# Seven inner products for the block product A12·B21 of an up-projection in one-level Strassen form

## The chip, the cores and the metric

The kernel runs on one core of a Trainium2 chip. The metric is the device time of one execution in microseconds: the median of three runs. The core's engines each run their own instruction stream: PE (TensorE, the matrix products), DVE (VectorE), ACT (ScalarE), POOL (GpSimd) and SP (SyncE, here the issuer of most DMAs). [...]

## The reference

One inference step of a hybrid streaming encoder layer, in float32: 1024 new frames of one stream (with 16 meta tokens ahead) and 32 frames of a running stream. What matters here is the feed-forward at the layer's end:

```python
def conv_ffn(x, gate_past, g, w_up, dw_w, dw_b, w_down):
    h = rmsnorm(x, g)
    u = h @ w_up                       # (tokens, 1024) @ (1024, 5632)
    gate, up = u[..., :D_FF], u[..., D_FF:]
    gate_ext = jnp.concatenate([gate_past, gate], axis=1)
    y = jax.nn.silu(depthwise_causal_conv(gate_ext, dw_w, dw_b)) * up
    return x + y @ w_down, gate_ext[:, -(FFN_CONV_WIDTH - 1):]
```

The gate passes a causal convolution of width 3 along the tokens, then silu, and multiplies the other half. D_FF is 2816, that is 22 tiles of 128 channels.

## The kernel before

**Products in float32.** Every factor is kept as two reduced-precision parts, `hi` (a cast) and `lo` (the rest, `raw - hi`), and a product is three matmuls into one PSUM bank: hi·hi, hi·lo, lo·hi. The helper `hilo` does such a split: a cast on ACT (line 1218), then a subtraction on DVE (line 1219). x after the second norm's weights is in `BH`, `BL`.

**Tiles.** The up-projection runs over f = 0 to 21, 128 channels of the gate and 128 of the other half each. Tiles 0 and 1 are plain products. From tile 2 on each tile is a 2 x 2 block product in Strassen's form (Winograd's variant): the weights' rows are the two halves (gate, other), their columns the two halves of the 1024 inputs; x is cut along the inputs and, within each of two parts of the tokens (p = 0, 1), into two blocks of tokens. Seven products instead of eight: product 1 is A11·B11, product 2 is A12·B21, and both add up to the gate of the first block of tokens; the rest use sums of blocks. `THI`, `TLO` hold the sums of x for products 5, 6, 7. Each product is done for both parts, so that a tile has 14 half products (q, p), each of 4 x 3 matmuls into a bank of 264 columns, or 268 for products 1 and 2 at p = 0 (four more tokens ahead of it). `SEQ_` gives the order 1, 5, 6, 2, 7, 3, 4; `BANK` puts products 1, 6, 7 and 4 one after the other into the same bank (they accumulate), 5 and 3 into a second, 2 into a third. After each half product its bank is added to one of the four blocks: the first write of a block is an ACT copy (line 1422), the later ones are DVE additions (line 1424). Tile 21 has the order `SEQL`: 1, 6, 7, 5, 3, 2, 4.

**Weights.** While tile f's products run, the generator `w_forms` prepares the weights of tile f + 1: it loads three pieces `b`, `a`, `g` (line 1244; 256, 256 and 512 KB), builds the sums on DVE (lines 1249, 1250, 1255, 1258) and splits each by `hilo` into buffers from the list `free`.

**The gate chain.** After product 3 of the second part, `gate_done` runs: a multiply on DVE (line 1338), two small POOL copies, a multiply-add (1341), two more (1344), silu on ACT (1347), a multiply (1348). `y_done` then multiplies with the other half (1353, 1354) and, for tiles 2 to 17, stores y and sums of its blocks for the down-projection (`t1` to `t4`, lines 1373 and 1381 to 1383; stores at 1365). Even tiles keep their gate in `X[2]` (in rows of the trace `x`, in rows of the program's order `x_2299`) and y in `rb`; odd tiles keep the gate in `gx` and y in `X[0]` (`x_2297`). `X[1]` (`x_2298`) holds the raw weights. `gate_start` (line 1334) writes two values of the state ahead of each tile on POOL.

**Order.** PE's order is that of the code. DVE, ACT, POOL and SP are ordered by a scheduler when the program is built.

**The step to the down-projection.** During tile 21 the function `first_hook` feeds what the first down-projection products (`d_mm`, lines 255 to 257 and 1625) read: y of tiles 0 and 1 (`arow`, into `th`, `tl`) and two blocks of `wdn`, `wa[1]` first needed and `wa[0]` needed later (both into `bh`, `bl`, 1024 columns). The loads are issued by the class `Feed` (line 1527), and each is split by `hilo`.

Of the kernel before, what the change touches and what calls it, by code (L numbers as in the profile page):

```python
# [169 lines left out]
def body(nc, tc, cp, wp, xp, dp, io):  # L170
# [1032 lines left out]
    with tc.tile_pool(name="psB", bufs=1, space=PSUM, reuse_waits="tile") as pf:  # L1203
# [34 lines left out]

        def w_forms(key, src, raws):
            w = ups[key] = Up()  # L1240
            g, a, b = raws
# [8 lines left out]
            tt_(out=a, in0=g[:, A], in1=a, op=ALU.subtract)  # L1250
# [99 lines left out]
        def y_done(f):  # L1350
# [134 lines left out]
        for i, (u, p, c) in enumerate(((0, 1, 0), (0, 1, 1), (0, 0, 0), (1, 1, 0), (1, 1, 1), (0, 0, 1), (1, 0, 0), (1, 0, 1))):  # L1485
# [3 lines left out]
            if i == 4:  # L1489
# [408 lines left out]
```

## Time and profile before

| | us |
|---|---|
| three timed runs: median (lowest to highest) | 1048.96 (1048.79 to 1049.0) |
| the profiled execution's own time | 1049.94 |
| its span, first to last instruction | 1048.2 |
| PE busy | 1030.8 |
| DVE busy | 864.8 |
| ACT busy | 506.6 |
| POOL busy | 163.0 |

The span is from the first to the last instruction of the profiled execution; its own time is that of the same execution as the timer gives it. The busy time of an engine is the sum of its instructions. The mean granted clock of TensorE was 0.999. Tile 2 begins at 393 us, tile 21 at 782, and the down-projection at 803.

### The profile page before, as it was taken

To read this page: it belongs to the slowest core of one execution; us is meant where nothing else is said; L and a number is where in the kernel's file an instruction comes from. 1 tells how busy PE (TensorE), PEld (TensorE's weight loads), DVE (VectorE), ACT (ScalarE), POOL (GpSimd) and SP (SyncE) were. 2 spreads that over 40 slices of the span, in tenths; PEclk is the share of its full clock that TensorE was granted. 3 is DMA by queue.
4 is the path that set the end of the run, shared out by engine and by line. 5 is a ranking of instruction groups with operands and counts; after the bars stand their busy time and mean duration, and the time that the engine had idled before them with its cause. 6 is when DMAs were issued, how large, how long until landed. Compare 5 with 4: busy or idle time off the path is not lost.

```text
span 1048.2 us, 19994 instructions
## 1 busy us (share of the span) xinstructions
PE 1030.8 (98%) x7747; PEld 1004.9 (96%) x7747; DVE 864.8 (83%) x1649; ACT 506.6 (48%) x1074; POOL 163.0 (16%) x205
## 2 busy tenths in 40 slices
PE   9999999989999999999999999999999999999997
PEld 8999998758999999999999999999999999999997
DVE  7999988899978978888887888888777976986636
ACT  8653336896676744433333443343336722532334
POOL 1133220002325220001000000110010041000043
PEclk9999999999999999999999999999999999999999
DMA  7378673124963123243233233332426795832204
GB/s 268 90 170 163 146 152 81 41 54 70 174 151 108 61 71 102 72 141 96 72 110 125 63 103 109 97 103 76 130 63 207 250 194 132 249 123 69 94 2 166
DMA packets 69047, 124.41 MB, mean 119 GB/s; under 512 B 10448, under 2 KB 42568, under 8 KB 68952
## 3 DMA queue, kind: packets, MB, share of 16 engines
q1 hardware_dynamic: 56392, 97.77, 29.2%
q0 software_dynamic: 12128, 24.95, 14.1%
q8 instruction: 61, 1.00, 0.4%
q10 hardware_dynamic: 432, 0.41, 0.1%
q14 instruction: 34, 0.28, 0.1%
HBM read 79.42 MB, written 27.51 MB: 102 GB/s over the span
## 4 chain that ended last, share of the span: by engine, by line
PE 88%; ACT 6%; DVE 3%; DMA 2%; issue 1%; DVEq 0%; ACTq 0%
PE mm L1282 55%; PE mm L255 10%; PE mm L256 10%; PE mm L257 10%; ACT pb L764 1%; DVE acc L403 1%; ACT glu L828 1%; DMA raw<-woc 1%; PE R L292 1%; ACT hi L341 1%; PE R L271 1%; DMA xs<-xT 0%; ACT glu L764 0%; ACT pb L774 0%; DMA prm<-prm 0%
## 5 line engine op out<-in xcount | busy, mean ns | idle before, releaser
L1282 PE MATMUL mm<-bh,sl 128*128 128x264 f32 (+1 forms) x912 | 214.0, 284 | 0.0
L1282 PEld LDWEIGHTS mm<-bh,sl 128*128 128x128 f32 x912 | 157.2, 188 | 0.0
L403 DVE SCALAR_TENSOR_TENSOR acc<-glu,prm,acc 128x324 f32<-128x324 f32 (+4 forms) x190 | 155.0, 844 | 1.1
L1282 PE MATMUL mm<-bl,sl 128*128 128x264 f32 (+1 forms) x424 | 120.9, 285 | 0.0
L1282 PE MATMUL mm<-th,rawr 128*128 128x264 f32 x640 | 120.0, 284 | 0.0
L1282 PE MATMUL mm<-bh,wlo 128*128 128x264 f32 (+1 forms) x440 | 117.6, 284 | 0.0
L1424 DVE TENSOR_TENSOR x<-x,mm 128x264 f32<-128x264 f32 (+7 forms) x238 | 76.5, 347 | 45.6 <-PE mm L1282 45.4
L1282 PE MATMUL mm<-bh,whi 128*128 128x264 f32 (+1 forms) x440 | 112.5, 284 | 0.0
L255 PE MATMUL mm<-hi,whi 128*128 128x352 f32 (+3 forms) x312 | 104.0, 333 | 0.0
L256 PE MATMUL mm<-lo,whi 128*128 128x352 f32 (+3 forms) x312 | 101.2, 324 | 0.2 <-DVE lo L342 0.2
L257 PE MATMUL mm<-hi,wlo 128*128 128x352 f32 (+3 forms) x312 | 101.2, 324 | 0.0
L1282 PEld LDWEIGHTS mm<-th,rawr 128*128 128x128 f32 x640 | 100.4, 188 | 0.0
L1282 PE MATMUL mm<-th,sl 128*128 128x264 f32 x352 | 92.7, 284 | 0.0
L1282 PE MATMUL mm<-tl,rawr 128*128 128x264 f32 x320 | 90.8, 284 | 0.0
L1282 PEld LDWEIGHTS mm<-bh,wlo 128*128 128x128 f32 x440 | 80.6, 188 | 0.0
L1282 PEld LDWEIGHTS mm<-bl,sl 128*128 128x128 f32 x424 | 79.9, 188 | 0.0
L1282 PEld LDWEIGHTS mm<-bh,whi 128*128 128x128 f32 x440 | 79.0, 188 | 0.0
L1282 PE MATMUL mm<-bl,whi 128*128 128x264 f32 (+1 forms) x272 | 77.5, 285 | 0.0
L1218 ACT CAST sl<-x 128x512 fp32r<-128x512 f32 (+1 forms) x41 | 29.7, 727 | 74.2 <-DMA x<-wup 41.0
L1282 PEld LDWEIGHTS mm<-th,sl 128*128 128x128 f32 x352 | 63.8, 188 | 0.0
L1282 PEld LDWEIGHTS mm<-tl,rawr 128*128 128x128 f32 x320 | 60.3, 188 | 0.0
L255 PEld LDWEIGHTS mm<-hi,whi 128*128 128x128 f32 x312 | 58.7, 188 | 1.2 <-issue 0.6
(400 smaller groups left out, 2923.1 us busy)
## 6 DMA issues: line engine op xcount, KB each, us to landing
x<-wup SPq DMA_DIRECT2D x20, 512.0 KB, 4.3
x<-wup SPq DMA_DIRECT2D x40, 256.0 KB, 2.8
yq<-x SPq DMA_DIRECT2D x32, 264.0 KB, 2.8
wlo<-raw POOLq DMA_DIRECT2D x16, 512.0 KB, 4.6
ca<-ca POOLq DMA_DIRECT2D x18, 383.0 KB, 5.2
raw<-win SPq DMA_DIRECT2D x12, 512.0 KB, 4.5
raw<-wdn SPq DMA_DIRECT2D x12, 512.0 KB, 4.6
rb<-yq SPq DMA_DIRECT2D x10, 528.0 KB, 5.0
```

Source lines behind the costliest of these rows:

```text
L255: nc.tensor.matmul(ps, whi(k), xhi(k), start=first and i == 0, stop=False)
L256: nc.tensor.matmul(ps, whi(k), xlo(k), start=False, stop=False)
L257: nc.tensor.matmul(ps, wlo(k), xhi(k), start=False, stop=last and i == n - 1)
L271: nc.tensor.matmul(ss[:, i:i + 1], z[:, at:at + P], ones[:, 0:1], start=j == 0, stop=j == len(parts) - 1)
L292: nc.tensor.matmul(R[:, at:at + P], left[i], diag[i], start=True, stop=True)
L341: hid[b, k] = nc.scalar.activation(HI[b][:, k, :], X[b][:, k, :], AF.Copy, scale=pcol("g1", k)).ins
L403: nc.vector.scalar_tensor_tensor(out=a, in0=e[:, a0 + k:a1 + k], scalar=pcol("cw", p * CW + k), in1=a, op0=ALU.mult, op1=ALU.add)
L764: nc.scalar.activation(qs_[i], qs_[i], AF.Exp, bias=m[0][:, i:i + 1], scale=-1.0, accum_out=m[1][:, i:i + 1])
L828: nc.scalar.copy(ptb[kv], pts[kv])
L1218: nc.scalar.copy(hi, raw)
L1282: nc.tensor.matmul(ps, w[:, j, :], x[:, j, :], start=first and j + i == 0, stop=j == 3 and i == 2, skip_group_check=True)
L1424: summed[0] = nc.vector.tensor_tensor(out=z, in0=z, in1=ps[:, lo_:hi_], op=ALU.add).ins
```

## The change

For the tiles 4 to 21 product 2 is no longer computed tile by tile. A pair of an even and the next odd tile shares B21, and the two tiles' A12 are the rows of a new 2 x 2 block matrix (tile f, tile f + 1; the two quarters of the inputs), B21 the other factor (the two quarters of the inputs, the two parts of the tokens). This is again done by seven products, the inner ones. Each has half the depth: 2 x 3 matmuls of 268 columns. All seven stand in the even tile (`level2`, steps `"L"`), between its twelve remaining half products; their results are added to the gates of both tiles, so the odd tile's gate has begun before its product 1, whose eviction becomes a DVE addition. The matmuls of a pair go from 336 to 330.

- *x*: in tiles 2 and 3 `x_level2` builds the sums of B21 for the inner products, in `XH`, `XL`, and overwrites the fourth inner block of x in `BH`, `BL` by its sum. It reads `BH`, `BL` by DMA into `X[1]`: an SP load of `BH` and an accumulating POOL transfer of `BL`.
- *weights*: of `g` only the first half (A11) is split per tile, in `w_part`: cast on ACT, negation on ACT, and the `lo` by an accumulating POOL transfer, instead of a DVE subtraction. `w_level2` builds the inner sums of the second halves of both tiles. The other tile's half is loaded early into `l2r` (256 KB more per pair, line 1270). Three buffers of the list `free` are kept for them. The yields of `w_forms` are spread by `L2AT`.
- *places*: `t2` and `t4` of the odd tiles go to `X[1]` instead of the gate buffer; `raws[0]` begins 16 columns later. `dynamic_dma_scratch_size=4096` is passed to the program.
- *tile 21*: no product 2; `gate_done` comes after product 3 as in the other tiles, and `wa[0]` is taken after product 4's first part.

```diff
+L2F, L2E = 4, NF
+L2SEQ = (1, 5, 6, 2, 3, 7, 4)
+L2AT = {"even": (1, 3, 5, 8, 10, 14, 16), "odd": (1, 3, 4, 5, 6, 7, 8, 9, 10, 11), "in": (2, 4, 5, 8, 9, 10, 11, 12, 12, 13)}
...
-    nc = bacc.Bacc("TRN2", target_bir_lowering=False, num_devices=1)
+    nc = bacc.Bacc("TRN2", target_bir_lowering=False, num_devices=1, dynamic_dma_scratch_size=4096)
...
+        def w_part(hi, lo, raw):
+            nc.scalar.copy(hi, raw)
+            nc.scalar.activation(lo, raw, AF.Copy, scale=-1.0)
+            nc.gpsimd.dma_start(lo, raw, accum_op=ALU.add)
...
+        def w_level2(g):
...
+            z = l2w[2]
+            hilo(z[:, 0:512], z[:, 512:1024], g)
+            tt_(out=l2q[:, 0:256], in0=g[:, 0:256], in1=l2r[:, 0:256], op=ALU.subtract)
+            tt_(out=l2r[:, 0:256], in0=l2r[:, 0:256], in1=l2r[:, 256:512], op=ALU.add)
+            tt_(out=l2q[:, 256:512], in0=l2r[:, 0:256], in1=g[:, 0:256], op=ALU.subtract)
+            tt_(out=l2s, in0=g[:, 256:512], in1=l2q[:, 256:512], op=ALU.subtract)
...
-            hilo(hg, lg, g)
+            if two:
+                w_part(hg[:, A], hg[:, B], g[:, A])
+            else:
+                hilo(hg, lg, g)
             yield
+            if two and key % 2 == 0:
+                w_level2(g[:, B])
+                yield
...
+            if two and key % 2 == 0:
+                for z, raw in zip(l2w, (l2r, l2q)):
+                    (hilo if key == L2F else w_part)(z[:, A], z[:, B], raw)
+                    yield
...
-            t2, t4, t3 = form_row(G), form_row(G, 2 * DN), form_row(Tm)
+            t2, t4, t3 = form_row(xf[1]), form_row(xf[1], 2 * DN), form_row(Tm)
...
+        def level2(f):
...
+            for q in L2SEQ:
...
+                for j in range(2):
+                    for z, x, i in ((hi, xh, 0), (hi, xl, 1), (lo, xh, 2)):
+                        nc.tensor.matmul(ps, z[:, j, :], x[:, j, :], start=q in FIRST and j + i == 0,
+                                         stop=j == 1 and i == 2, skip_group_check=True)
+                row, p = OUT[q]
+                ps = ps[:, L2N - PNS[p] - HALO[p]:]
+                for lo_, hi_, z in dsts[row](0, 0, p):
+                    if q in (4, 5):
+                        nc.scalar.copy(z, ps[:, lo_:hi_])
+                    else:
+                        nc.vector.tensor_tensor(out=z, in0=z, in1=ps[:, lo_:hi_], op=ALU.add)
+                yield
...
+        even = [z for z in pairs if z[0] != 2]
+        for i in (4, 6, 8, 10, 12, 14, 16):
+            even.insert(i, ("L", 0))
+        even[16], even[17] = even[17], even[16]
+        odd = [z for z in pairs if z[0] != 2]
...
-            if q == 2 and p:
+            if q == 4 and not p:
                 feeda.take(keep=False)
                 feed.stages += [x1a, x2a]
                 feed.fill()
 
-        run(up_strassen(NF - 1, [(q, p) for q in SEQL for p in range(2)]), None, first_hook)
+        run(up_strassen(NF - 1, [(q, p) for q in SEQL if q != 2 for p in range(2)]), None, first_hook)
```

The even tile's half products become (1,0) (1,1) (5,0) (5,1) L1 (6,0) L5 (6,1) L6 (7,0) L2 (7,1) L3 (3,0) L7 (3,1) (4,0) L4 (4,1), the odd tile's (1,0) (1,1) (5,0) (5,1) (6,0) (6,1) (7,0) (7,1) (3,0) (3,1) (4,0) (4,1).

Lines move with the change. In the changed program 1223 and 1224 are the cast and subtraction of `hilo`, 1245 to 1247 `w_part`, 1258 to 1261 the sums of `w_level2`, 1278 to 1293 the sums of `w_forms`, 1332 the block products, 1541 the inner products, 1476 and 1478 the evictions by ACT and DVE, 1547 and 1549 those of the inner products, 1388 to 1398 the gate chain.

Three places show how the engines' order moves. The first is ACT in an odd tile, from the eviction of (5,0) into y (`x_2297`) to the two pieces of (6,1) into the gate (`gx_3660`). Before:

```order
L1422 COPY x_2297<-mm 128x264
L1218 CAST rawr<-x_2298 128x512
L1422 COPY x_2297<-mm 128x264
L1347 ACTIVATE x_2299<-x_2299 128x1058
L1422 COPY gx_3660<-mm 128x264
L1218 CAST rawr<-x_2298 128x512
L1422 COPY gx_3660<-mm 128x232
L1422 COPY gx_3660<-mm 128x32
```

With the change, the same stretch:

```order
L1476 COPY x_2297<-mm 128x264
L1397 ACTIVATE x_2299<-x_2299 128x1058
L1245 CAST sl<-x_2298 128x512
L1246 ACTIVATE sl<-x_2298 128x512
L1476 COPY x_2297<-mm 128x264
L1223 CAST rawr<-x_2298 128x512
L1245 CAST sl<-x_2298 128x512
L1246 ACTIVATE sl<-x_2298 128x512
L1476 COPY gx_3660<-mm 128x264
L1476 COPY gx_3660<-mm 128x232
L1476 COPY gx_3660<-mm 128x32
```

Between the copies of (5,0) and (6,0) stood one cast, a copy and silu; now there are two casts with their negations, another cast, the copy and silu.

The second is DVE at the passage from an even to an odd tile: the gate chain of the even tile (gate in `x_2299`) and the preparation of the next even tile's weights. Before:

```order
L1249 TENSOR_TENSOR x_2298<-x_2299,x_2298 128x512
L1338 TENSOR_TENSOR x_2299<-x_2299,rbg 128x1060
L1250 TENSOR_TENSOR x_2299<-x_2298,x_2299 128x512
L1219 TENSOR_TENSOR sl<-x_2298,whi 128x1024
L1341 TENSOR_SCALAR x_2299<-x_2299,prm 128x1058
L1344 SCALAR_TENSOR_TENSOR x_2299<-x_2299,prm 128x1058
L1219 TENSOR_TENSOR wlo<-x_2299,whi 128x512
L1344 SCALAR_TENSOR_TENSOR x_2299<-x_2299,prm 128x1058
```

With the change:

```order
L1388 TENSOR_TENSOR x_2299<-x_2299,rbg 128x1060
L1391 TENSOR_SCALAR x_2299<-x_2299,prm 128x1058
L1394 SCALAR_TENSOR_TENSOR x_2299<-x_2299,prm 128x1058
L1258 TENSOR_TENSOR x_2298<-x_2298 128x256
L1224 TENSOR_TENSOR sl<-x_2298,sl 128x512 x2
L1394 SCALAR_TENSOR_TENSOR x_2299<-x_2299,prm 128x1058
L1478 TENSOR_TENSOR gx_3660<-gx_3660,mm 128x268
L1259 TENSOR_TENSOR x_2298<-x_2298 128x256
L1278 TENSOR_TENSOR x_2298<-x_2299,x_2298 128x512
L1478 TENSOR_TENSOR gx_3660<-gx_3660,mm 128x264
```

The gate chain is closer together at its start, and its last multiply stands behind the first inner sum and two subtractions of `hilo`; then come the evictions of the odd tile's (1,0) and (1,1), which are additions now.

The third is DVE at the end of tile 21, where the blocks of `wdn` are split into `bl` (128x4x256: first `wa[0]`, then `wa[1]`). Before:

```order
L1424 TENSOR_TENSOR gx_3660<-gx_3660,mm 128x264
L1219 TENSOR_TENSOR bl<-x_2298,bh 128x4x256
L1424 TENSOR_TENSOR gx_3660<-gx_3660,mm 128x232
L1424 TENSOR_TENSOR gx_3660<-gx_3660,mm 128x32
L1219 TENSOR_TENSOR bl<-x_2298,bh 128x4x256
L1424 TENSOR_TENSOR gx_3660<-gx_3660,mm 128x268
L1424 TENSOR_TENSOR gx_3660<-gx_3660,mm 128x264
L1219 TENSOR_TENSOR bl<-x_2299,bh 128x4x264
L1338 TENSOR_TENSOR gx_3660<-gx_3660,rbg 128x1060
```

With the change:

```order
L1478 TENSOR_TENSOR gx_3660<-gx_3660,mm 128x264
L1224 TENSOR_TENSOR bl<-x_2298,bh 128x4x256
L1478 TENSOR_TENSOR gx_3660<-gx_3660,mm 128x232
L1478 TENSOR_TENSOR gx_3660<-gx_3660,mm 128x32
L1224 TENSOR_TENSOR bl<-x_2299,bh 128x4x264
L1388 TENSOR_TENSOR gx_3660<-gx_3660,rbg 128x1060
L1224 TENSOR_TENSOR bl<-x_2298,bh 128x4x256
L1391 TENSOR_SCALAR x_2297<-gx_3660,prm 128x1058
```

The two evictions of product 2 are gone, and the split of a block of y (`bl<-x_2299`) and the first multiply of the gate chain stand ahead of the second block of `wdn` instead of behind it.

More of the change, by code (lines that the diff above doesn't have):

```diff
@@ L101 @@
 HALO = (NMETA - H0, 0)
+L2F, L2E = 4, NF
+L2N = PNS[0] + HALO[0]
+XAT = {2: ((1, 0), (2, 0), (2, 1), (4, 0)), 3: ((1, 0), (1, 1), (2, 1))}
+L2SEQ = (1, 5, 6, 2, 3, 7, 4)
+L2AT = {"even": (1, 3, 5, 8, 10, 14, 16), "odd": (1, 3, 4, 5, 6, 7, 8, 9, 10, 11), "in": (2, 4, 5, 8, 9, 10, 11, 12, 12, 13)}
 DN = 264
@@ L1244, in w_forms @@
                 nc.sync.dma_start(z, y)
+            if isinstance(key, int) and key % 2 == 0 and L2F <= key < L2E:
+                nc.sync.dma_start(l2r, up_src(key + 1, 0)[:, B])
             yield
-            a22, hg, lg, h12, l12, h34, l34 = (free.pop(0) for _ in range(7))
+            two = isinstance(key, int) and L2F <= key < L2E
+            if key == L2F:
+                free[:] = [free[i] for i in (0, 1, 3, 4, 5, 6, 7, 8, 2, 9)]
+            a22, hg, lg, h12, l12, h34, l34 = (None if two and i == 2 else free.pop(0) for i in range(7))
             tt_ = nc.vector.tensor_tensor
@@ L1407, in body, with strassen @@
         summed, gated = [None], [None]
-        def strassen(key, steps, dst, ns, halo=(0, 0), fresh=True):
-            banks, begun = {}, set()
+        def strassen(key, steps, dst, ns, halo=(0, 0), fresh=True, pre=(), inner=None):
+            banks, begun = {}, set(pre)
             for q, p in steps:
+                if q == "L":
+                    next(inner)
+                    yield q, p
+                    continue
                 k = p, BANK[q]
@@ L1427, in up_strassen @@
         def up_strassen(f, steps):
             gate_start(f)
-            for q, p in strassen(f, steps, up_dst(f), PNS, HALO):
-                if (q, p) == (3 if f < NF - 1 else 2, 1):
+            two = L2F <= f < L2E
+            pre = [((0, 0), p) for p in range(2)] if two and f % 2 else ()
+            for q, p in strassen(f, steps, up_dst(f), PNS, HALO, True, pre, level2(f) if two and not f % 2 else None):
+                if (q, p) == (3, 1):
                     gate_done(f)
@@ L1494, in body @@
                 sl = [sl[:, i * 1024:i * 1024 + 1024] for i in range(4)]
+                XH, XL = (new(pr, z, 3, 2, L2N, dt=F32R) for z in ("xh", "xl"))
                 rawr = [wp.tile([P, 1024], F32R, tag="raw", name="rawr") for _ in range(2)]
@@ L1577, in body @@
         STEPS = [(c, mp) for c in range(2) for mp in (3, 2, 1, 0)]
-        for f in range(2, NF - 1):
-            run(up_strassen(f, pairs), w_forms(f + 1, up_srcs(f + 1), raws))
+        even = [z for z in pairs if z[0] != 2]
[3 more added lines that the diff above has]
+        odd = [z for z in pairs if z[0] != 2]
+        forms2 = x_level2()
+        for f in range(2, NF - 1):
+            kind = "even" if f % 2 == 0 else "odd"
+            steps = even if f % 2 == 0 else odd
+            hook = None
+            if not L2F <= f < L2E:
+                steps = pairs
+            if f < L2F:
+                hook = lambda q, p: next(forms2, None) if (q, p) in XAT[f] else None
+            at = (1, 3, 5, 7, 9, 11, 13)
+            if f + 1 == L2F:
+                at = L2AT["in"]
+            elif L2F <= f < L2E:
+                at = L2AT[kind]
+            run(up_strassen(f, steps), w_forms(f + 1, up_srcs(f + 1), raws), hook, at)
         wa = [form(3, p, 2 * P) for p in range(2)]
```

69 lines of the change are left out of this document (68 added, 1 removed).

## The prediction

> **What bounds the kernel now.** I read the profile page first: the busy shares, then the shares of the chain of work that ended last.
>
> ```profile
> PE 1030.8 (98%) x7747; PEld 1004.9 (96%) x7747; DVE 864.8 (83%) x1649; ACT 506.6 (48%) x1074; POOL 163.0 (16%) x205
> ...
> PE 88%; ACT 6%; DVE 3%; DMA 2%; issue 1%; DVEq 0%; ACTq 0%
> PE mm L1282 55%; PE mm L255 10%; PE mm L256 10%; PE mm L257 10%; ACT pb L764 1%; DVE acc L403 1%; ACT glu L828 1%; DMA raw<-woc 1%; PE R L292 1%; ACT hi L341 1%; PE R L271 1%; DMA xs<-xT 0%; ACT glu L764 0%; ACT pb L774 0%; DMA prm<-prm 0%
> ```
>
> TensorE is the bound, and the products of line 1282 are 55% of the chain. But these are averages over the whole program, so I looked at the changed stage alone, with the view that sums each engine over a window:
>
> ```profile
> 550.00:600.00 50.00, 50.00 (x412) 50.00 (x411) 40.65 (x64) 18.17 (x37) 4.05 (x8) 1.00 0.32 100
> ```
>
> PE is busy for all 50 us at a granted clock of 1.00; DVE for 40.65, ACT for 18.17. So a matmul taken out is time taken out, as long as the engines that empty PSUM still come in time. To price a matmul I need a steady pitch. The small POOL copy at line 1334 stands once per tile at a fixed phase; of the even tiles these are the first and the last of seven in that stretch (tiles 8 and 20), and beside them are the first matmuls of three half products:
>
> ```profile
> 501.61 0.18 POOL L1334 COPY x<-prm 128x2 f32<-128x2 f32 x1 [4.02 <-DVE x L1344]
> ...
> 747.17 0.18 POOL L1334 COPY x<-prm 128x2 f32<-128x2 f32 x1 [4.02 <-DVE x L1344]
> ```
> ```profile
> 545.40 0.29 PE L1282 MATMUL mm<-bh,sl 128*128 128x268 f32 x1
> ...
> 546.89 0.28 PE L1282 MATMUL mm<-bh,sl 128*128 128x264 f32 x1
> ...
> 548.36 0.28 PE L1282 MATMUL mm<-th,wlo 128*128 128x264 f32 x1
> ```
>
> Six pairs take 747.17 - 501.61 = 245.56 us, so a pair takes 40.93 and a tile 20.46. Its 168 matmuls come every 0.122 us. Twelve at 268 columns take 1.49, twelve at 264 take 1.47.
>
> **What PE saves.** A pair loses four half products, 2 x (1.49 + 1.47) = 5.92 us, and gains 7 x 6 = 42 matmuls at 268 columns, 42 x 1.49 / 12 = 5.21. That is 0.71 per pair, 0.70 by the mean pitch; I take 0.705. All 42 stand in the even tile: it grows to 20.46 - 2.96 + 5.21 = 22.71, and the odd one shrinks to 17.5. The gain is small because seven inner products of six matmuls replace 48 matmuls. Eight pairs (4 to 19) give **-5.64 us**. The ninth pair splits: tile 20 is longer by **+2.25**; what tile 21's -2.96 is worth is decided at its end, below.
>
> **The odd tile: a new wait.** In an odd tile, PE took product 2 between products 6 and 7. Product 7 accumulates in the PSUM bank of product 6, so (7,0) must wait until ACT has copied (6,0) out. Before, three half products lay between; now only (6,1). Counted from the odd tile's first matmul, (6,0) ends at 1.49 + 4 x 1.46 = 7.33 and PE wants to begin (7,0) at 8.79. On ACT, by the order of the changed program, stand after the copy of (5,0): silu of the even tile, a cast and a negation, the copy of (5,1), two casts and a negation, and then the copy of (6,0). The pitch of each is read from consecutive starts, and the negation from the group of line 244, which at 1024 columns costs what a cast of that size does (1.05):
>
> ```profile
> 542.64 0.62 ACT L1218 CAST rawr<-x 128x512 fp32r<-128x512 f32 x1 [1.03 <-PE mm L1282]
> 543.16 0.37 ACT L1422 COPY x<-mm 128x264 f32<-128x264 f32 x1
> 543.43 1.09 ACT L1347 ACTIVATE x<-x 128x1058 f32<-128x1058 f32 x1
> 544.42 0.37 ACT L1422 COPY gx<-mm 128x264 f32<-128x264 f32 x1
> ```
> ```profile
> L244 ACT ACTIVATE wlo<-raw x15: 1050/1057/1076, 27.4 to 270.0; 128x1024 fp32r<-128x1024 f32 x15
> ```
>
> Cast 0.52, copy 0.27, silu 0.99, negation 0.53. The delay from PE to ACT is about 0.2:
>
> ```profile
> 558.76 0.38 ACT L1422 COPY x<-mm 128x268 f32<-128x268 f32 x1 [1.10 <-PE mm L1282]
> ...
> 557.09 0.28 PE L1282 MATMUL mm<-bh,sl 128*128 128x268 f32 x1
> ```
>
> (the product that begins at 557.09 ends 1.48 later, at 558.57, and its copy starts at 558.76). So (5,0) ends at 4.41 and its copy starts at 4.61; silu at 4.88, then 5.87, 6.39, 6.92 (copy of (5,1)), 7.19, 7.71, 8.23, and the copy of (6,0) runs from 8.76 to 9.14. With the hand-over PE goes on at 9.2 to 9.3 instead of 8.79: a wait of 0.35 to 0.55.
>
> That holds if silu's input is there by 4.88. It comes from DVE, where the last multiply of the gate chain (old line 1344) now stands behind the first sum of the inner weights (new line 1258) and two `lo` subtractions, and that sum needs the 512 KB load of the next weights. By the DVE pitches
>
> ```profile
> 555.93 1.25 DVE L1338 TENSOR_TENSOR gx<-gx,rbg 128x1060 f32<-128x1060 f32 x1
> 557.10 0.68 DVE L1250 TENSOR_TENSOR x<-x,x 128x512 f32<-128x512 f32 x1
> ...
> 558.84 0.82 DVE L1341 TENSOR_SCALAR x<-gx,prm 128x1058 f32<-128x1058 f32 x1
> 559.70 1.32 DVE L1344 SCALAR_TENSOR_TENSOR x<-gx,prm,x 128x1058 f32<-128x1058 f32 x1
> 560.94 0.69 DVE L1219 TENSOR_TENSOR sl<-x,sl 128x512 fp32r<-128x512 f32 x1
> 561.54 1.31 DVE L1344 SCALAR_TENSOR_TENSOR x<-gx,prm,x 128x1058 f32<-128x1058 f32 x1
> ```
>
> (1.17, 0.86, 1.24 and 0.60) the gate chain, which starts after (3,1) is emptied at -3.1 and a `lo` of 0.60, reaches line 1258 at about +0.8. The load's buffer is released by that same `lo` at -2.5, so it is issued at about -2.2. It takes 4.3:
>
> ```profile
> x<-wup SPq DMA_DIRECT2D x20, 512.0 KB, 4.3
> ...
> DMA to landing us min/median/max: 2.6/2.8/5.0
> ```
>
> It lands at +2.1. Then 0.35 (an estimate from the 0.34 of an eviction of 264 columns), 2 x 0.60 and 1.24 bring the input to +4.9 or 5.0, 0.1 behind 4.88. I take **0.5 us** per odd tile; eight odd tiles from 5 to 19 make **+4.0**. Behind PE's wait stand only its own products. Behind line 1258 on DVE stand also the evictions of (1,0) and (1,1), whose banks PE takes again at 5.87 and 7.33; by the same pitches they are done at about 5.4 and 6.6. The ends are 0 (the copy comes in time after all) and 1.3 (the load lands at 5.0, the latest of line 1244).
>
> **The end of tile 21: a wait in place of the gain.** The first products of the down-projection use the second block of `wdn`, cast and subtracted into `bh` and `bl`. On ACT its cast stands behind that of the first block, whose load is issued late:
>
> ```profile
> 792.38 0.38 SPq L1527 DMA_DIRECT2D x<-wdn  x1
> ...
> DMA to landing us min/median/max: 3.5/3.7/6.1
> ```
> ```profile
> 797.67 1.05 ACT L1218 CAST bh<-x 128x1024 fp32r<-128x1024 f32 x1 [2.17 <-DMA x<-wdn]
> 798.63 0.62 ACT L1218 CAST whi<-raw 128x512 fp32r<-128x512 f32 x1
> 799.15 1.04 ACT L1218 CAST bh<-x 128x1024 fp32r<-128x1024 f32 x1
> ```
> ```profile
> 798.75 1.23 DVE L1219 TENSOR_TENSOR bl<-x,bh 128x1024 fp32r<-128x1024 f32 x1 [1.62 <-ACT bh L1218]
> 799.90 0.48 DVE L1424 TENSOR_TENSOR gx<-gx,mm 128x232 f32<-128x232 f32 x2
> 800.30 1.22 DVE L1219 TENSOR_TENSOR bl<-x,bh 128x1024 fp32r<-128x1024 f32 x1
> ...
> 802.12 1.25 DVE L1219 TENSOR_TENSOR bl<-x,bh 128x1056 fp32r<-128x1056 f32 x1
> 803.29 1.25 DVE L1338 TENSOR_TENSOR gx<-gx,rbg 128x1060 f32<-128x1060 f32 x1
> ```
> ```profile
> 782.30 0.28 PE L1282 MATMUL mm<-bl,sl 128*128 128x268 f32 x1
> ...
> 802.61 0.34 PE L255 MATMUL mm<-th,bh 128*128 128x384 f32 x1
> 802.79 0.34 PE L256 MATMUL mm<-tl,bh 128*128 128x384 f32 x1
> 802.96 0.34 PE L257 MATMUL mm<-th,bl 128*128 128x384 f32 x1
> ```
>
> Tile 21 begins one matmul ahead of the row at 782.30, at 782.17. The first cast starts 15.5 us into the tile, and the second `bl` is done at 801.52, 19.35 in; the third matmul needs it at 20.79. Product 2 was part of what covered this. Now PE is through with the tile at 17.5. The load is released by work in the tile's first half, which stays, so the casts don't move: the second `bh` is done at about 18.0, and two matmuls can run. On DVE the order now puts the `bl` of 1056 columns (1.17) and the start of the gate chain (line 1338, 1.17) ahead of that second `bl`: 15.5 + 1.08 + 1.15 + 0.40 + 1.17 + 1.17 + 1.22 = 21.69. So the third matmul starts at about 21.75 instead of 20.79: PE idles some 3.9 us and tile 21 with its junction costs **+0.95** instead of -2.96. Were the load to land in 3.7 us, the median of that line's loads, it would be -0.6; at their longest, 6.1, it would be +1.9.
>
> **What is hidden, and at what price.** In tiles 2 and 3 the block sums of x are built: some 14 small DVE operations in two groups, ACT casts, POOL transfers. At 0.35 each one group is about 2.5 us of DVE. PE had no wait there, and DVE idles for some of that time; I charge **+0.1**, between 0 and 2. Per pair DVE gains seven inner evictions (some 1.9 us), four sums and two `lo` (2.4) and two evictions in place of ACT copies (0.7), and loses two `lo` of 1024 columns (2.3) and product 2's evictions (1.5): +1.2 us, against 40.65 busy of 50. ACT gains about 3 us per pair beside 18.17 of 50. Only where PE waits for one of them by order, as above, does that count. The weights that now go through POOL's accumulating transfer,
>
> ```profile
> wlo<-raw POOLq DMA_DIRECT2D x16, 512.0 KB, 4.6
> ```
>
> take 4.6 us at twice the size, and are used over 10 us later. The sums of y in their new place free `gx` earlier and shorten nothing on PE.
>
> **Sum.** -5.64 + 4.0 + 2.25 + 0.95 + 0.1 = +1.66 us on the profiled execution's 1049.94, that is 1051.6; the three timed runs have their median 0.98 lower, at 1048.96, so the forecast is **1050.6**.
>
> **The rivals.**
> - *ACT comes in time.* The odd wait rests on a margin of half a microsecond in an 8 us queue; the order of that queue is certain, its times are not. At 0 to 0.2 us per tile the time is 1046.6 to 1048.2; with a faster landing at the junction, from 1045.0 on.
> - *Neither wait.* The junction's load would have to come 3 us sooner, which the row at 792.38 speaks against: 1048.96 - 5.64 + 2.25 - 2.96 + 0.1 = 1042.7.
> - *Slower: the 512 KB load decides the odd tile.* From a landing of 4.2 us on, each 0.1 us more is 0.1 us on eight tiles, since line 1258 holds up the gate chain, silu and so the copy of (6,0). The median is already 4.3; a new 256 KB load stands just ahead of it on SP's queue. At 5.0 the wait is 1.3: 1050.6 + 8 x 0.8 = 1057.0.
> [...]
>
> **How the numbers follow.** Forecast 0.48 (odd waits of 0.25 to 0.8, so 1048.6 to 1053.0); ACT in time 0.24; neither wait 0.07; slow load 0.18; clock 0.03. The range 1045.0 to 1055.5 leaves out the case without waits and the upper half of the slow loads. A measurement can tell about 0.2%, 2.1 us: faster is below 1046.9, slower above 1051.1. Faster: 0.20 of ACT in time and 0.07, 0.27. Slower: 0.14 of the forecast, 0.18 and 0.03, 0.35. Same: the rest, 0.38.
>
> **What would show it.** Of the changed profile: POOL's copies of the even tiles about 40.7 apart (40.2 without odd waits, 41.5 with slow loads); in each odd tile a PE idle time of about 0.5 released by ACT's copy of (6,0); tile 20 at 22.7; a PE idle time of 3 to 4 us ahead of the third matmul of the down-projection, released by DVE's `bl`; PE's clock there. A PE wait inside an even tile, at an inner product or its bank, or one in tiles 2 to 4, would prove the walk wrong, and so would an order in which the `bl` isn't last.

## The result and the profile after

| | before | after |
|---|---|---|
| median of six runs each (lowest to highest), us | 1048.98 (1048.72 to 1049.34) | 1056.29 (1055.09 to 1060.35) |
| ratio, with its 95% interval | | 1.0074 (1.0057 to 1.0091) |
| the profiled execution's own time, us | 1049.94 | 1055.93 |
| its span, us | 1048.2 | 1053.7 |
| mean granted clock of TensorE | 0.999 | 0.994 |

The change makes the kernel 0.74% slower; the forecast was 1050.6, with a range up to 1055.5. What follows is read from the two profiled executions, whose spans differ by 5.50 us while the medians differ by 7.31: the profiled execution of before took 0.96 more than its median, that of the changed kernel 0.36 less, and 0.5 lies outside the spans. The busy shares and the chain of waits on the page of the changed kernel, to be held against the first fence of the prediction:

```profile
PE 1029.7 (98%) x7693; PEld 1001.2 (95%) x7693; DVE 882.0 (84%) x1730; ACT 540.6 (51%) x1154; POOL 192.2 (18%) x247
...
PE 80%; ACT 9%; DVE 6%; DMA 3%; issue 1%; SPq 0%; DVEq 0%; POOL 0%; ACTq 0%; POOLq 0%
PE mm L1332 43%; PE mm L260 10%; PE mm L262 10%; PE mm L261 10%; PE mm L1541 4%; ACT pb L769 1%; DVE acc L408 1%; ACT glu L833 1%; ACT x L1397 1%; ACT sl L1246 1%; ACT sl L1245 1%; PE R L1541 1%; DMA x<-bl 1%; PE R L297 1%; DVE x L1394 1%
```

54 matmuls are gone (7747 to 7693), and PE's share of the chain fell from 88 to 80%: the chain now runs through work that was hidden. New in it are ACT's silu, cast and negation (lines 1397, 1245, 1246) and `DMA x<-bl`, the accumulating transfer of `x_level2`. PE's waits between 370 us and the end (waited for, us in total, times, longest) say where; the same view of before is empty:

```profile
PE mm L1332 <- DVE rb L1478: 2.5, 1, 2.5
PE mm L262 <- DVE bl L1224: 2.0, 1, 2.0
PE mm L1332 <- ACT gx L1476: 1.8, 8, 0.2
PE mm L260 <- ACT bh L1223: 0.2, 1, 0.2
```

The third line is the forecast wait of the odd tiles (the odd wait), eight times; the second and fourth are the forecast wait at the step to the down-projection (the junction). The first, inside tile 2, was not forecast. To place the loss I cut both spans at ACT's eviction of an even tile's (1,0), which comes 1.7 us behind the tile's first matmul in both kernels. Timeline of ACT (start, duration), before in tiles 2, 6 and 20:

```profile
395.06 0.38 ACT L1422 COPY x<-mm 128x268 f32<-128x268 f32 x1 [0.58 <-PE mm L1282]
...
476.94 0.38 ACT L1422 COPY x<-mm 128x268 f32<-128x268 f32 x1 [1.11 <-PE mm L1282]
...
763.42 0.38 ACT L1422 COPY x<-mm 128x268 f32<-128x268 f32 x1 [1.12 <-PE mm L1282]
```

and after:

```profile
394.03 0.38 ACT L1476 COPY x<-mm 128x268 f32<-128x268 f32 x1
...
479.98 0.38 ACT L1476 COPY x<-mm 128x268 f32<-128x268 f32 x1 [0.70 <-PE mm L1332]
...
764.98 0.38 ACT L1476 COPY x<-mm 128x268 f32<-128x268 f32 x1 [0.70 <-PE mm L1332]
```

The last cut is the third matmul of the down-projection, at 802.96 before (a row of the prediction) and 806.81 after (shown below). Stretches in us:

| stretch | before | after | difference | forecast |
|---|---|---|---|---|
| start to tile 2 | 395.06 | 394.03 | -1.03 | 0 |
| tiles 2 to 5 | 81.88 | 85.95 | **+4.07** | -0.1 |
| tiles 6 to 19, seven pairs | 286.48 | 285.00 | -1.48 | -1.44 |
| tile 20 to the third matmul | 39.54 | 41.83 | +2.29 | +3.20 |
| third matmul to the end | 245.24 | 246.89 | **+1.65** | 0 |
| span | 1048.2 | 1053.7 | +5.50 | +1.66 |

The first row's difference is not the change's: ACT's cast behind the load of `woc` starts at 302.48 before and at 301.44 after, and the first new transfer is issued only at 357.12. The sums of the first half of x stand in this row too; DVE idled 1.16 us ahead of them, and PE waited nowhere between 340 us and tile 2. The steady part came out as forecast; the whole miss is in two rows, tiles 2 to 5 and the stretch behind the junction.

**Tile 2.** The timelines of PE, DVE, POOL and SP of the changed kernel, read backwards from the wait (in brackets the idle time and its releaser; the fence goes from the wait to its source):

```profile
409.81 0.28 PE L1332 MATMUL mm<-bh,whi 128*128 128x264 f32 x1
412.58 0.39 PE L1332 MATMUL mm<-bh,sl 128*128 128x264 f32 x1 [2.49 <-DVE rb L1478]
```
```profile
396.92 1.31 DVE L1394 SCALAR_TENSOR_TENSOR x<-gx,prm,x 128x1058 f32<-128x1058 f32 x1
403.60 0.16 DVE L1496 TENSOR_TENSOR x<-x 128x4 f32<-128x4 f32 x1 [5.37 <-DMA x<-bl]
...
412.11 0.42 DVE L1478 TENSOR_TENSOR rb<-rb,mm 128x264 f32<-128x264 f32 x1
```
```profile
396.06 2.44 POOL L1493 DMA_DIRECT2D x<-bl  x2 [3.96 <-DMA x<-bh]
```
```profile
392.89 1.47 SPq L1492 DMA_DIRECT2D x<-bh  x2
```

SP loads the second half of x from `BH` at 392.89; POOL waits 3.96 for it and then issues two accumulating transfers of `BL`; the first sum on DVE waits for those until 403.60, and DVE stands idle for 5.37 us. All that DVE has queued behind, the gate chain and the evictions included, comes late: the eviction that PE waits for starts at 412.11, where before it started at 407.47 in a program that was 1.03 behind:

```profile
407.47 0.42 DVE L1424 TENSOR_TENSOR rb<-rb,mm 128x264 f32<-128x264 f32 x1
```

PE had some slack and loses 412.58 - 409.81 - 0.12 = 2.65 us. Then its clock falls. Windows of 2 us (busy time of PE, PEld, DVE, ACT, POOL, then granted clock, DMA share, GB/s):

```profile
412.00:414.00 2.00, 1.42 (x11) 1.42 (x12) 2.00 (x6) 0.62 (x1) 0.00 (x0) 0.95 0.98 137
414.00:416.00 2.00, 2.00 (x11) 2.00 (x11) 2.00 (x7) 0.90 (x2) 0.00 (x0) 0.50 0.17 57
416.00:418.00 2.00, 2.00 (x13) 2.00 (x13) 2.00 (x4) 1.00 (x2) 0.74 (x1) 0.69 0.59 205
```

PE shows busy there, but the last two windows hold 11 and 13 matmuls where the windows at 1.00 beside them (404 to 410, 418 to 422) hold 18 or 19: the granted clock is 0.50 and 0.69. That is an estimated 2 x (0.05 + 0.50 + 0.31) = 1.7 us, and with 2.65 it is 4.4, of which the pair of tiles 4 and 5 gives 0.2 back. Whether the 1.7 is a loss of its own is asked in the next run.

**The odd wait.** PE and ACT in one odd tile of the changed kernel, around (7,0):

```profile
591.08 0.28 PE L1332 MATMUL mm<-th,rawr 128*128 128x264 f32 x1
591.59 0.39 PE L1332 MATMUL mm<-th,whi 128*128 128x264 f32 x1 [0.23 <-ACT gx L1476]
591.82 0.29 PE L1332 MATMUL mm<-tl,whi 128*128 128x264 f32 x1
```
```profile
587.03 0.38 ACT L1476 COPY x<-mm 128x264 f32<-128x264 f32 x1 [0.42 <-PE mm L1332]
587.30 1.09 ACT L1397 ACTIVATE x<-x 128x1058 f32<-128x1058 f32 x1
...
591.17 0.73 ACT L1476 COPY gx<-mm 128x264 f32<-128x264 f32 x3
```

The wait shows 0.23 of idle time, but from 591.08 to 591.82 two matmuls take 0.74 instead of 0.24: it costs 0.50. In the same trace matmuls of 0.28 start 0.12 apart (590.48, 590.60), so they overlap; behind this wait the overlap is missing, and the first one takes 0.39. The view of waits adds only the idle time. ACT's queue from the copy of (5,0) runs without a gap, with silu at once behind that copy, and DVE had silu's input ready at 586.6, 0.7 earlier: it is ACT's length, not the load behind line 1258, that decides.

**The junction.** PE, ACT and SP at the end of tile 21, which began at 785.99:

```profile
803.69 0.28 PE L1332 MATMUL mm<-bh,wlo 128*128 128x264 f32 x1
804.17 0.44 PE L260 MATMUL mm<-th,bh 128*128 128x384 f32 x1 [0.19 <-ACT bh L1223]
804.45 0.34 PE L261 MATMUL mm<-tl,bh 128*128 128x384 f32 x1
806.81 0.69 PE L262 MATMUL mm<-th,bl 128*128 128x384 f32 x1 [2.02 <-DVE bl L1224]
```
```profile
800.57 1.05 ACT L1223 CAST bh<-x 128x1024 fp32r<-128x1024 f32 x1 [2.09 <-DMA x<-wdn]
```
```profile
796.20 0.38 SPq L1655 DMA_DIRECT2D x<-wdn  x1
```

The load is issued 10.2 us into the tile, as before (792.38 - 782.17), and its cast starts 4.37 behind the issue instead of 5.29. (`L1655` is the changed program's line 1527.) From 806.81 on the matmuls are long (0.69, then 0.52, where before, at a clock of 1.00, they took 0.34), and the clock is low until about 810 (0.59 in the window from 806, 0.56 in the next); then it is back:

```profile
808.00:810.00 2.00, 2.00 (x9) 2.00 (x8) 2.00 (x2) 1.39 (x3) 0.00 (x0) 0.56 0.78 263
810.00:812.00 2.00, 2.00 (x14) 2.00 (x13) 2.00 (x3) 1.81 (x3) 0.00 (x0) 1.00 0.90 251
```

### The profile page after: what moved, and what is told of

Its sections match the earlier page's. It is cut to its first block, busy times and chain, and to the rows that moved or that the text cites. A ratio compares the mean times of both kernels' runs of the same rounds, so it can differ in the third digit from the quotient of the medians.

```text
span 1053.7 us, 20165 instructions
## 1 busy us (share of the span) xinstructions
PE 1029.7 (98%) x7693; PEld 1001.2 (95%) x7693; DVE 882.0 (84%) x1730; ACT 540.6 (51%) x1154; POOL 192.2 (18%) x247
## 4 chain that ended last, share of the span: by engine, by line
PE 80%; ACT 9%; DVE 6%; DMA 3%; issue 1%; SPq 0%; DVEq 0%; POOL 0%; ACTq 0%; POOLq 0%
PE mm L1332 43%; PE mm L260 10%; PE mm L262 10%; PE mm L261 10%; PE mm L1541 4%; ACT pb L769 1%; DVE acc L408 1%; ACT glu L833 1%; ACT x L1397 1%; ACT sl L1246 1%; ACT sl L1245 1%; PE R L1541 1%; DMA x<-bl 1%; PE R L297 1%; DVE x L1394 1%
## 5 line engine op out<-in xcount | busy, mean ns | idle before, releaser
L1332 PE MATMUL mm<-bh,whi 128*128 128x264 f32 (+1 forms) x584 | 140.4, 285 | 0.0
L1332 PE MATMUL mm<-bl,whi 128*128 128x264 f32 (+1 forms) x368 | 105.0, 285 | 0.0
L1332 PE MATMUL mm<-bh,sl 128*128 128x264 f32 (+1 forms) x472 | 99.9, 287 | 2.5 <-DVE rb L1478 2.5
L1332 PEld LDWEIGHTS mm<-bh,whi 128*128 128x128 f32 x584 | 102.0, 189 | 0.2 <-DVE x L1478 0.2
L1332 PE MATMUL mm<-th,whi 128*128 128x264 f32 x280 | 80.4, 287 | 1.8 <-ACT gx L1476 1.8
L1332 PEld LDWEIGHTS mm<-bh,sl 128*128 128x128 f32 x472 | 78.8, 191 | 2.7 <-DVE rb L1478 2.7
L1332 PE MATMUL mm<-bl,sl 128*128 128x264 f32 (+1 forms) x272 | 78.0, 287 | 0.0
L1332 PEld LDWEIGHTS mm<-bl,whi 128*128 128x128 f32 x368 | 69.2, 188 | 0.0
L1223 ACT CAST whi<-x 128x512 fp32r<-128x512 f32 (+1 forms) x37 | 23.4, 633 | 84.6 <-PE mm L1332 81.9
L261 PEld LDWEIGHTS mm<-lo,whi 128*128 128x128 f32 x312 | 58.8, 188 | 0.6 <-DVE lo L347 0.4
```

The costliest lines, as they stand in the source:

```text
L261: nc.tensor.matmul(ps, whi(k), xlo(k), start=False, stop=False)
L1223: nc.scalar.copy(hi, raw)
L1332: nc.tensor.matmul(ps, w[:, j, :], x[:, j, :], start=first and j + i == 0, stop=j == 3 and i == 2, skip_group_check=True)
```

## The experiments

Runs are listed with their median and with the ratio to the kernel before, timed beside them (its median was 1048.97 to 1049.32). The stretches of the table above are read from each run's trace.

**again**: the changed kernel once more, beside the next three.

> The changed kernel once more, as the standard for the three beside it. Theory: the loss is made at two places, a PE wait of 2.5 us in tile 2 and one of about 2.2 us ahead of the down-projection, each followed by some 3.5 us at half the clock; it repeats, so both waits and both stretches of 0.5 clock show again and the time lies between 1055 and 1060. Rival: they were an accident of one execution; then they are missing here or stand elsewhere.

1056.65, ratio 1.0073 (1.0058 to 1.0088). Junction and half clock behind it came again (0.50 in the windows from 807.62 to 810.62, third matmul to the end 247.08). Tile 2 differs: the wait is there, the half clock isn't:

```profile
412.42 0.39 PE L1332 MATMUL mm<-bh,sl 128*128 128x264 f32 x1 [2.25 <-DVE rb L1478]
```
```profile
414.00:416.00 2.00, 2.00 (x19) 2.00 (x18) 2.00 (x6) 1.00 (x3) 0.00 (x0) 1.00 0.34 93
```

Still tiles 2 to 5 took 86.24, no less than 85.95: PE now idles 0.32, 0.40 and 0.73 us in three windows of 4 us in tiles 3 to 5 (424 to 428, 464 to 472), where after the half clock it idled 0.23 in all, the odd wait of tile 5. So the slow clock seems to have filled time in which DVE was late anyhow. Two runs below keep this tile 2 as it is: `junction_first` took 86.10 for tiles 2 to 5, `odd_late` (wait of 2.89) 85.25.

**entry_late**: the six DVE sums of the second half of x are placed behind `summed[0]`, the last DVE eviction of tile 2.

```diff
-                tt_(out=h, in0=h, in1=b22[:, 0:e], op=ALU.add)
+                with tc.issue_after(summed[0]) if r else nullcontext():
+                    tt_(out=h, in0=h, in1=b22[:, 0:e], op=ALU.add)
...
```

> Only the DVE sums of the second half of x for the inner products are held back until tile 2's products are emptied, so that nothing of tile 2 waits behind the POOL transfer that they need. Theory: PE's wait of 2.5 us in tile 2 and the half clock behind it (1.7) go, the even tiles from tile 2 to tile 4 are 41.0 apart instead of 45.2, and the time falls by 4.2 us against the changed kernel run beside it. Rival: DVE has too much work in tiles 2 and 3 in any case; then the wait moves to tile 3 and most of the 4.2 stays.

1058.23, ratio 1.0088 (1.0073 to 1.0103): no better. The fall of 4.2 us that was expected did not come; the rival did, in tile 4 rather than tile 3, with 87.23 for tiles 2 to 5. The wait in tile 2 is gone, but the sums keep `X[1]` occupied, into which the odd tile's half of the weights (`l2r`) is loaded, and SP issues that load at 432.00 instead of 414.48. DVE and PE of this kernel:

```profile
435.18 0.42 DVE L1258 TENSOR_TENSOR x<-x 128x256 f32<-128x256 f32 x1 [4.94 <-DMA x<-wup]
```
```profile
441.44 0.39 PE L1332 MATMUL mm<-th,rawr 128*128 128x264 f32 x1 [1.11 <-ACT x L1476]
...
446.78 0.39 PE L1542 MATMUL mm<-xh,sl 128*128 128x268 f32 x1 [1.42 <-DVE x L1550]
...
449.19 0.39 PE L1332 MATMUL mm<-th,whi 128*128 128x264 f32 x1 [1.41 <-ACT x L1476]
```

DVE's stop of 4.94 us takes the place of that of 5.37. Moving the consumers does not help while the transfer is as late as it is.

**no_low_part**: the two accumulating transfers of the second half of x are left out.

```diff
-                    nc.gpsimd.dma_start(st[:, i], l2_blocks(BL, 4 + r + 2 * i), accum_op=ALU.add)
+                    if not r:
+                        nc.gpsimd.dma_start(st[:, i], l2_blocks(BL, 4 + r + 2 * i), accum_op=ALU.add)
```

> The two accumulating POOL transfers for the second half of x (its low part) are left out, so those sums are made of the high part alone; all else stays. Theory of the late transfer: they land 7 us after their issue and hold DVE from 398 to 403.6, and all of tile 2 behind it; without them the sums start at about 398, no PE wait is left in tiles 2 to 5, tiles 2 to 6 take 81.7 to 82.5 us instead of 86.0 (86.2 in the repetition), and the time falls by 3.5 to 4.5 us against the changed kernel (1056.5). Rival: tiles 2 and 3 hold too much work for DVE and for the loads behind it; then the waits only move and tiles 2 to 6 still take over 85.

1052.75, ratio 1.0030 (1.0021 to 1.0040). The first of the sums on DVE (here line 1497) starts without a wait, 6.7 us ahead of the 403.60 above:

```profile
396.86 0.16 DVE L1497 TENSOR_TENSOR x<-x 128x4 f32<-128x4 f32 x1
```

Tiles 2 to 5 take 81.64, 4.3 less than after, and PE's wait in tile 2 is gone; the time fell by 3.9 against `again`, as expected. Nothing else was changed, so the accumulating transfer is what the entry's loss hangs on; the SP load stayed.

**dve_sums**: the same sums of `BH` and `BL` made by two DVE additions instead of load and transfer; nothing is left out.

```diff
+                    if r:
+                        tt_(out=st[:, i], in0=l2_blocks(BH, 4 + r + 2 * i), in1=l2_blocks(BL, 4 + r + 2 * i), op=ALU.add)
+                        continue
```

> Inner products from tile 4 as in the change, but the second half of x is put together on DVE (two additions of 536 columns, 0.7 us each) instead of by SP loads and POOL's accumulating transfers; nothing is left out. Theory: what crowds tiles 2 and 3 is the transfer's 7 us, not DVE's work, so even with 1.4 us more of DVE work the PE wait in tile 2 goes, tiles 2 to 6 take 81.6 to 82.2 us and the time falls by 3.4 to 4.4 us against the changed kernel (1056.5). Rival: the run that left the low part out was quick because it had less to do; then 1 to 3 us of waits come back and tiles 2 to 6 take over 83.

1053.24, ratio 1.0036 (1.0022 to 1.0050). Tiles 2 to 5 take 477.01 - 395.29 = 81.72. The price is two DVE rows:

```profile
393.40 0.72 DVE L1493 TENSOR_TENSOR x<-bh,bl 128x536 f32<-128x536 f32 x1
...
394.64 0.71 DVE L1493 TENSOR_TENSOR x<-bh,bl 128x536 f32<-128x536 f32 x1
```

1.43 us of DVE replace 5.37 us of DVE waiting, and the rival, that leaving out work had made `no_low_part` quick, is gone.

**fill_gaps**: 18 matmuls without use ahead of (4,0) in tile 2, and 12 ahead of the down-projection, to keep PE from idling; the order of some DVE and ACT work in tiles 3 to 5 moved with them.

```diff
+                if (key, q, p) == (2, 4, 0):
+                    busy = pf.tile([P, 512], F32, tag="nm", name="R", bufs=2)[:, :264]
+                    for _ in range(18):
+                        nc.tensor.matmul(busy, ups[2].prod[3][0][:, 0, :], form(3, 0, 264)[0][:, 0, :], start=True, stop=True)
...
+            if i == 0:
...
+                for _ in range(12):
+                    nc.tensor.matmul(busy, arow[0][0][:, 0:P], arow[0][0][:, 0:384], start=True, stop=True)
```

> Both waits stay, but PE spends them on matmuls whose result is not used: 18 at 264 columns in tile 2 (2.2 us), 12 at 384 ahead of the down-projection (2.1 us). Theory of the clock: no idle time of over 0.5 us is left, the clock stays at 1.00 at both places, and the time falls by 3.0 to 3.4 us though nothing arrives earlier. Rival: what is lost behind the waits is a backlog of DVE and ACT, not the clock; then the time stays within 1 us of the changed kernel's.

1059.8, ratio 1.0102 (1.0087 to 1.0117): slower still, 3.2 above `again`, where the theory expected 3.0 to 3.4 less and its rival no change. The wait in tile 2 shrinks to 0.51 at a clock of 1.00, and the lateness shows up in tile 3 and again at the junction. PE of this kernel:

```profile
410.18 2.33 PE L1474 MATMUL R<-bh,sl 128*128 128x264 f32 x18
413.01 0.39 PE L1332 MATMUL mm<-bh,sl 128*128 128x264 f32 x1 [0.51 <-DVE rb L1482]
...
426.04 0.39 PE L1332 MATMUL mm<-th,rawr 128*128 128x264 f32 x1 [2.25 <-ACT gx L1480]
...
812.22 0.46 PE L262 MATMUL mm<-th,bl 128*128 128x384 f32 x1 [1.82 <-DVE bl L1224]
```

Half clock follows both of the long waits: the windows from 424 to 428 and from 428 to 432 show 0.85 and 0.72, and at the junction the matmuls of 384 columns start 0.29 to 0.32 apart behind the wait, 0.17 ahead of it. At the entry this speaks, as `again` did, against the clock as the cause: DVE's lateness sets the time. At the junction the 12 matmuls ran ahead of the two that were not held up, so the gap only moved; whether a filled junction would keep the clock is not answered.

**junction_first**: the taking of `wa[0]` and the gate chain of tile 21 are placed behind the cast and the subtraction of `wa[1]`.

```diff
-                if (q, p) == (3, 1):
+                if (q, p) == (3, 1) and f < NF - 1:
...
-                feeda.take(keep=False)
+                with tc.issue_after(block1[0]), tc.issue_after(block1[1]):
+                    feeda.take(keep=False)
+                    gate_done(NF - 1)
...
-                with tc.issue_after(gated[0]):
+                with tc.issue_after(gated[0]), tc.issue_after(block1[0]):
```

> Only the end of tile 21: the block of wdn that the down-projection needs first is cast and subtracted ahead of the other block and of the gate chain. Theory: PE's wait there shrinks from 2.2 us to under 0.5 and the clock stays at 1.00, so the time falls by 3.3 to 3.8 us against the changed kernel; the step from tile 20 to the third matmul of the down-projection is 39.7 to 40.2 instead of 41.8. Rival: the transfers bound the junction; then the wait stands at another matmul within the next 10 us and the time falls by under 1.5.

1051.66, ratio 1.0021 (1.0012 to 1.0031), 5.0 less than `again`. PE runs through the junction:

```profile
804.37 0.34 PE L260 MATMUL mm<-th,bh 128*128 128x384 f32 x1
804.55 0.34 PE L261 MATMUL mm<-tl,bh 128*128 128x384 f32 x1
804.72 0.34 PE L262 MATMUL mm<-th,bl 128*128 128x384 f32 x1
```

Tile 20 to the third matmul takes 39.15 (41.83 after, 42.28 in `again`), and from there to the end 245.18 (246.89 after, 247.08 in `again`, 245.24 before). Against the changed kernel's profile that is 2.7 and 1.7 us, against `again` 3.1 and 1.9: the wait and the half clock that came of it. It is more than the 3.3 to 3.8 expected. With the wait gone the clock stays up: the matmuls of 384 columns behind the junction take 0.34, here and in `all_mended`.

**odd_late**: the splits of the inner weights (two casts and negations on ACT) are placed behind the copy of (6,0).

```diff
-                    (hilo if key == L2F else w_part)(z[:, A], z[:, B], raw)
+                    with tc.issue_after(emptied[6, 0]) if key > L2F else nullcontext():
+                        (hilo if key == L2F else w_part)(z[:, A], z[:, B], raw)
...
-                        nc.scalar.copy(z, ps[:, lo_:hi_])
+                        emptied[q, p] = nc.scalar.copy(z, ps[:, lo_:hi_]).ins
```

> In the odd tiles from 5 on the casts and negations of the inner weights stand behind ACT's copy of (6,0) instead of ahead of it. Theory: each PE wait costs 0.5 us (0.23 shown as idle, the rest is draining and starting the pipeline), so without it the even tiles are 40.22 to 40.30 apart instead of 40.71 and the time falls by 3.3 to 3.9 us. Rival: only the idle time shown counts; then the pitch is 40.48 and the time falls by 1.8.

1053.94, ratio 1.0049 (1.0034 to 1.0063). The pitch of a pair falls from 285.00 / 7 = 40.71 to 40.47, half of the 0.5: the wait at (7,0) is gone and a smaller one stands at (7,1), for the copy of (6,1), behind which the splits had not been put. PE's matmuls show no idle time there, its weight loads (PEld) between 480 and 760 us do:

```profile
PEld mm L1333 <- ACT gx L1478: 1.3, 7, 0.2
```

From start to start two weight loads at (7,1) take 0.48 (591.68 to 592.16) instead of 0.24. The pitch is the number that the rival had named (40.48, only the shown idle time counts), but not for the rival's reason: with the second wait gone too it falls to 40.22 (`all_mended`).

**from_tile_6**: the new form begins with tile 6 (one pair fewer), with the sums of x spread over tiles 2 to 5 and the edit of `entry_late`.

```diff
-L2F, L2E = 4, NF
+L2F, L2E = 6, NF
...
-XAT = {2: ((1, 0), (2, 0), (2, 1), (4, 0)), 3: ((1, 0), (1, 1), (2, 1))}
+XAT = {2: ((1, 0), (2, 0), (2, 1), (4, 0)), 3: ((1, 0), (1, 1)), 4: (), 5: ((2, 1),)}
```

> The inner products begin with tile 6 instead of tile 4, tiles 4 and 5 keep product 2, and the sums of the second half of x are made after tile 2's products are emptied. Theory: with two more tiles for the preparation nobody waits for it; tiles 2 to 6 take 81.9 to 82.4 us (81.88 in the kernel before), and the time falls by 3.6 to 4.3 us against the changed kernel, one pair's 0.2 us given up. Rival: the start of the inner weights is what crowds DVE and ACT, wherever it stands; then 2 to 5 us of waits show in tiles 5 and 6.

1053.93, ratio 1.0052 (1.0037 to 1.0066). Tiles 2 to 5 take 82.55, so the room helps where the mere move did not; but they hold no pair of the new form, and the plain tiles took 81.88. The gain, some 2.6 us, is less than the 3.6 to 4.3 expected. At the junction the profiled execution, the slowest of the four, had a wait of 3.05 in one piece (up to 806.09) and half clock in the three windows behind it, and the stretch to the end was the longest of all, 248.21:

```profile
806.00:808.00 2.00, 1.91 (x6) 1.91 (x7) 2.00 (x4) 1.30 (x2) 0.79 (x3) 0.50 0.44 80
808.00:810.00 2.00, 2.00 (x9) 2.00 (x8) 2.00 (x2) 0.72 (x3) 0.00 (x0) 0.50 0.91 270
810.00:812.00 2.00, 2.00 (x8) 2.00 (x7) 2.00 (x3) 1.44 (x2) 0.00 (x0) 0.50 0.54 215
```

**three_mended**: the edits of `from_tile_6`, `junction_first` and `odd_late` together.

> The three edits together: inner products from tile 6, the first needed block of wdn first at the junction, the inner weights behind the copy of (6,0). Theory: the places are independent, so the gains add up: 1056.5 - 4.0 - 4.8 - 3.1 = 1044.6, which is 0.4% faster than before; the pitch is 40.22 to 40.30, the clock 1.00 from tile 2 to the down-projection. Rival: with PE's waits gone another engine, DVE at 88 to 90% or the loads, sets the pitch; then it stays at 40.5 or above and the time is 1046.5 or more.

1047.09, ratio 0.9980 (0.9971 to 0.9989): faster than before, but 2.5 above the 1044.6 expected. A pair takes 40.50 where 40.22 to 40.30 was expected, some 2 us on eight pairs; the weight loads are not without idle time (busy 49.80 of the 50 us from 550 to 600, 50.00 in `all_mended`). These are the numbers of the rival (another engine sets the pitch); `all_mended` speaks against its reason. From the third matmul to the end it took 245.32, against 245.24 before.

**all_mended**: all pairs from tile 4, with the edits of `dve_sums` and `junction_first`, and the splits of the inner weights behind the copy of (6,1) instead of (6,0).

> All three places mended, all nine pairs kept: x put together on DVE, the first needed block of wdn first, and in the odd tiles the inner weights behind both copies of product 6 (behind the first copy alone, a wait of 0.24 was left at (7,1)). Theory: without any wait the pitch is the sum of the matmuls, 66 at 0.1234 and 264 at 0.1216, 40.24; the time is 1056.5 - 4.0 - 4.8 - 3.8 = 1043.9, 0.5% faster than before. Rival: with the casts later, the next even tile waits for its inner weights, or DVE falls behind; then the pitch stays at 40.4 or more and the time is over 1045.5.

1044.8 (1043.8 to 1045.35), ratio 0.9958 (0.9944 to 0.9971), beside 1048.97: the best of all, 0.9 above the 1043.9 expected. In the stretch of the first window of the prediction PE is never idle, and from 370 us on the view of PE's waits has one row left:

```profile
550.00:600.00 50.00, 50.00 (x413) 50.00 (x412) 43.50 (x72) 22.61 (x48) 6.66 (x14) 1.00 0.52 143
```
```profile
PE mm L1548 <- DVE x L1556: 0.6, 1, 0.6
```

The pitch of a pair is 40.22, 0.71 below the 40.93 of before. The one wait left stands in tile 20, where an inner product waits for a DVE eviction; from there to the third matmul it took 39.97, against 39.15 in `junction_first`.

## Why the prediction missed

- **What PE saves, 0.705 per pair: right.** With the waits gone a pair is 0.71 shorter (`all_mended`). (The 0.70 "by the mean pitch" is not six matmuls at 0.122, which are 0.73; nothing hangs on it.)
- **The odd tile's wait, 0.5: right, in size and cause.** 0.50 from start to start; seven pairs gained 1.48 where 7 x 0.205 = 1.44 was forecast. `odd_late` moved it by moving ACT's splits. The walk of ACT's queue came out to the hundredth: counted from the odd tile's first matmul at 582.42, the copies of (5,0) and (6,0) start at 4.61 and 8.75, forecast 4.61 and 8.76. Only the last 0.1, taken from a late load, has another source, the slower start behind a wait. The slow-load rival did not come: silu started directly behind the copy of (5,0).
- **The junction, +2.25 and +0.95: the mechanism right, one term too long.** The order on DVE was as read, and `junction_first` shows it to be the cause. The working took the load's 5.29 us of before; it measured 4.37 in this execution, so the third matmul stood 806.81 - 785.99 = 20.82 into the tile, 0.03 later than before rather than 0.95. That is the luck of one execution: PE's wait for the cast was 0.19 here, 0.7 in `again` and 0.8 in `dve_sums`, whose junction is the same, and from tile 20 to the third matmul `entry_late` took 41.96 and `again` 42.28, 0.2 and 0.5 later than before. The bounds of -0.6 to +1.9 (by the prediction's own rows +1.8) had all of this inside.
- **"What is hidden", +0.1, between 0 and 2: wrong, and this is the step that failed.** Tiles 2 to 5 lost 4.1, and without the transfer (`no_low_part`) or with DVE sums in its place (`dve_sums`) nothing. The step added up the DVE instructions of the new sums and set them against DVE's idle time. It did not follow what those sums wait for: an SP load, then POOL's transfer on the same buffer, 403.60 - 392.89 = 10.7 us from end to end; and not what stands behind the first of them in DVE's order, the evictions that PE needs. It had listed POOL transfers, and counted them as hidden because a weight transfer elsewhere had 10 us to spare; here nothing was known of the spare time, and the upper bound of 2 had no row behind it.
- **The clock, a chance of 0.03: it fell.** From the third matmul to the end it took 1.65 us more than before, and `junction_first` without a gap 0.06 less. The forecast held a gap of 3.9 us; the wait came out shorter, in two pieces (0.19 and 2.02), and still the clock fell, as it did after 1.82 us of idle with 2 us of matmuls just ahead (`fill_gaps`). The 0.03 was the author's estimate; no row of before shows the clock falling in a gap. The longest PE wait in the trace of before was 1.68 us, at 306.26, and the clock stayed at 1.00 behind it; nothing there spoke of longer ones, so a chance of 0.03 was too little.

Row by row of the table, the forecast sum of +1.66 becomes 1.66 + (4.07 + 0.1) + 1.65 + (2.29 - 3.20) - 0.04 - 1.03 = 5.50, the difference of the spans (the -0.04 is that of the seven pairs, the -1.03 the stretch ahead of tile 2).

## What to carry to other kernels

A new operation can cost what it waits for, not what it takes (here 5.37 us of waiting ahead of an addition of 0.16, with the evictions queued behind it): follow its inputs back to the first DMA and look what is queued behind it, before calling it hidden. At a passage between two stages, have what is needed first prepared first; there an order on DVE cost 2.7 us, and the clock that fell after it 1.7 more. A small sum between two buffers on chip may be cheaper on the busy engine (1.43 us of DVE here) than by transfers that leave that engine waiting (5.37).

## What the runs showed of the hardware

- **Short gaps can halve the clock.** Half clock followed the wait at the junction in `after`, `again`, `dve_sums` and `from_tile_6` (its longest piece 2.0 to 3.05 us, windows of 0.50 behind it) and in `fill_gaps` (1.82), the wait in tile 2 in `after` (2.49, 0.50 behind it), and the one in tile 3 of `fill_gaps` (2.25). It did not follow the wait in tile 2 in `again` (2.25, 1.00 behind it). The length alone does not decide, and one program did both at one place. What does is not settled here. A stretch of half clock lasted some 3.4 us in tile 2 of `after` and at the junction of `again` and `dve_sums`, some 6.0 behind the wait in `from_tile_6`; from the third matmul to the end, against before, it cost 1.7 (`after`) to 3.0 us (`from_tile_6`).
- **A wait can cost more than its idle time**: in the odd tile of `after` 0.23 shown, 0.50 from start to start; and 0.24 at (7,1) in `odd_late` by the starts of the weight loads, where the matmuls show none.
- **The accumulating transfers arrived late**: from POOL's issue of two at 396.06 to DVE's release at 403.60 it took 7.5 us, for 268 KB each. The median from issue to landing was 4.9 for the four of them in `after`.
